# Hybrid decoder layer on one core: two gate blocks kept in SBUF, four product and four x loads moved to SP's queue, reciprocals three steps apart, cross-attention evicted by head pair

## The chip, the core and the metric

The kernel runs on one core of one Trainium2 chip. The core has a matrix engine (TensorE, in the profile PE, with PEld for its weight loads), three engines for elementwise work (VectorE or DVE, ScalarE or ACT, GpSimd or POOL) and SyncE (SP), which in this kernel only issues transfers. Transfers between HBM and the on-chip memory SBUF run on 16 transfer engines, whichever engine issues them. TensorE writes to PSUM, eight banks of 2 KB per partition, from where ScalarE and VectorE read.

The metric is the device time of one execution in microseconds (us). Before the change the median of three runs is 2236.44 us (2235.84 to 2237.41).

## The reference

One decoder layer in float32 over 256 tokens of width 2048: a SwiGLU feed-forward block, a gated mixer of windowed attention and RWKV-7 time mixing, cross-attention into a memory of 256 tokens, and a second feed-forward block. What the change touches:

```python
def gated_parallel_mixer(x, ...):
    p = rms_norm(x, norm_g) @ w_in
    q, k, v, p_rwkv, gates = jnp.split(p, c, axis=-1)
    y_attn = sliding_window_attention(q, k, v, sinks)
    y_rwkv = rwkv7_time_mix(p_rwkv, mu, ...)
    gate_attn, gate_rwkv = jnp.split(jax.nn.sigmoid(gates), 2, axis=-1)
    merged = gate_attn * (y_attn @ w_proj_attn) + gate_rwkv * (y_rwkv @ w_proj_rwkv)
    return x + merged @ w_out

def rwkv7_time_mix(...):
    kk = k * k_k
    kk = kk / jnp.maximum(jnp.sqrt(jnp.sum(kk * kk, axis=-1, keepdims=True)), 1e-12)
    ...

def memory_cross_attention(x, mem, ...):          # 4 heads of 128
    pr = jax.nn.softmax(s, axis=-1)
    o = jnp.einsum('bhtm,bmhd->bthd', pr, vm).reshape(B, T, CROSS_WIDTH)
    return x + o @ w_o
```

## The kernel before

**Products.** Each large product multiplies 256 tokens with a weight matrix in columns of 512. To keep float32 accuracy, every operand is split in a rounded part `hi` and a rest `lo`, and each block is multiplied three times: `hi` by `hi` (L422), weight `lo` by activation `hi` (L423), weight `hi` by activation `lo` (L424). Weights come in blocks of two rows of 128 by 512 columns (512 KB) through four buffers `raw`: SP issues the load (L322), ScalarE casts it to `hi` (L330), VectorE subtracts to get `lo` (L331). Up to four blocks are loaded ahead and two are split ahead. A product with 2048 rows has eight such blocks, one on `yr` has four.

**Background work.** Everything beside the large products is written as generators, kept in named groups (`ew`, `chain`, `norm`, `feat`, `mem` and others). `product` calls `bg.tick()` after every six matmuls, and a tick takes each group's first generators one step further; `yield from idle(n)` lets n ticks pass. So the text of the program interleaves background work with the matmuls. From this text a scheduler makes the order of instructions on each engine and chooses the buffers, so that an instruction may stand ahead of one written earlier.

**The mixer stage.** All its intermediate tiles share 20 buffers of 4 KB per partition (`t4`), among them the halves of `yr`, `mt` and the memory's activations, and the tiles `gr`, `gl`, `ml` and `x2` below. In order of the text: the products for keys; for each of four blocks of 512 columns an attention gate and the projection of the attention's output, whose product is stored to HBM (`md`, L1205); the rows for RWKV; four gate blocks of RWKV (L1520 to L1525), each put through a sigmoid into `gr` and stored to HBM (`grd`); four blocks of the RWKV projection on `yr` (L1535 to L1544), where GpSimd loads back the gate (`gl`, L1537) and the attention's product (`ml`, L1538), and VectorE multiplies and adds them (L1541, L1542); four blocks of the output product (L1558 to L1562), where GpSimd loads a block of x (`x2`, L1559) to which the product is added.

Stores and loads of these tiles are all issued by GpSimd, in its own order; the weights have SP's queue for themselves.

**The key's norm.** `removal_keys(h)` in group `ew`, for each half `h` of the RWKV heads: squares, sums by matmul (L1112), a square root on ScalarE (L1113), then on VectorE a maximum (L1115), four reciprocals of 128x256 (L1117) with two ticks between them (L1118), and the product with `kk` (L1119), followed by a tick (L1120). After it, in the same generator, come the scaled keys (L1123 to L1141) and two blocks of products stored to HBM (L1160). Behind both halves in the same group stands `substitute`, 31 steps of a triangular inverse on VectorE (L1177, L1182), whose result is stored (L1184) and loaded back for `invert` (L1269 to L1273). `chain(h)` and `finish(h)` need it and give `yr`.

**Cross-attention.** The weighted sum over the memory is eight matmuls into one two-bank tile `b4` (L1617 to L1621): for each half of the memory, four heads of 256 columns, so that heads 0 and 1 lie in one bank and 2 and 3 in the other. Then `split` (L634 to L638) is called for each pair of heads: a cast on ScalarE (L636) and a subtraction on VectorE (L637). The product with the output weights needs both.

Of the kernel before, what the change touches and what calls it, by code (L numbers as in the profile page):

```python
# [15 lines left out]
P = 128  # L16
# [124 lines left out]
def decoder_layer(ctx: ExitStack, tc: tile.TileContext, a: dict, out: bass.AP):  # L141
    nc = tc.nc
    act, dve, pool, pe = nc.scalar, nc.vector, nc.gpsimd, nc.tensor
# [17 lines left out]
    def f32(x):  # L161
        return x.bitcast(F32)
# [4 lines left out]
    def two():  # L167
        return ps.tile([P, 2, 512], F32, tag="two", name="two", bufs=2)

    def by_turns(products, late=False):  # L170


        prev = newest["pe"] if late else None
        for to, lhs, rhs, *flags in products:
            how = flags[0] if flags else dict(start=True, stop=True)
            with tc.issue_after(prev.ins) if prev else nullcontext():
                prev = pe.matmul(to, lhs, rhs, **how)  # L177
# [9 lines left out]
    def wait_for(name):  # L187
        while name not in bg.seen:
            yield

    def idle(n):
        for _ in range(n):
            yield
# [86 lines left out]
    for entry in weight_plan(a):  # L280
# [4 lines left out]
        w, k0, nk, c0, n = entry  # L285
# [348 lines left out]
    def split(x: Act, c, n, src):  # L634

        act.copy(x.at(0, c, n), src)  # L636
        dve.tensor_tensor(x.at(1, c, n), src, f32(x.at(0, c, n)), ALU.subtract)  # L637
        x.done |= set(range(c, c + n))  # L638
# [143 lines left out]
    def blk(d, n):  # L782
        return d[:, n * 512 : (n + 1) * 512].rearrange("(t p) n -> p t n", p=P)

    W = {n: v[0] for n, v in a.items() if n not in _LAID}
    x1d = dram.tile([T, D], F32, name="x1d")
    x3d = dram.tile([T, D], F32, name="x3d")
    md = dram.tile([T, D], F32, name="md")
    grd = dram.tile([T, D], F32, name="grd")
# [59 lines left out]
    with tc.tile_pool(name="mx", bufs=1, reuse_waits="tile") as sp:  # L849
        aligned(sp)  # L850

        def t4(name, shape=(P, 4, T), dt=F32):
            return sp.tile(list(shape), dt, tag="t4", name=name, bufs=N4)
# [173 lines left out]
        def halves(x):  # L1027
            return x[:].rearrange("p c (b t) -> p (c b) t", b=2)
# [69 lines left out]
        def removal_keys(h):  # L1098
            yield from wait_for(f"k{h}")
            yield from wait_for("decay")  # L1100
            ei = cs[h]
            kk, sq = t4("kk"), t4("sq")
            for i in range(4):
                c = 4 * h + i
                act.activation(kk[:, i, :], kt[h][:, i, :], AF.Copy, scale=nk_k[:, c : c + 1])
            yield
            act.activation(sq[:], kk[:], AF.Square)
            yield
            b = two()
            v = sq[:].rearrange("p (a c) t -> p a (c t)", a=2)  # L1110
            for i in range(2):
                pe.matmul(b[:, i], bdones[:], v[:, i], start=True, stop=True)  # L1112
            act.activation(v, b[:], AF.Sqrt)  # L1113
            yield
            dve.tensor_scalar(sq[:], sq[:], 1e-12, None, ALU.max)  # L1115
            for i in range(4):
                dve.reciprocal(sq[:, i, :], sq[:, i, :])  # L1117
                yield from idle(2)  # L1118
            dve.tensor_tensor(kk[:], kk[:], sq[:], ALU.mult)  # L1119
            yield  # L1120
            at_.append(t4("at"))
            for later, before in ((slice(1, P), ee[h][:, :, : P - 1]), (0, e0[h][:])):
                dve.scalar_tensor_tensor(  # L1123
                    halves(at_[h])[:, :, later], halves(kk)[:, :, later], DOWN, before,
                    ALU.mult, ALU.mult,
                )
            yield
            dve.scalar_tensor_tensor(kk[:], kk[:], -1.0, aa[h][:], ALU.mult, ALU.mult)
            yield
            dve.tensor_tensor(kk[:], kk[:], ei[:], ALU.mult)  # L1130
            bt.append(kk)
            yield
            for i in range(4):
                c = 4 * h + i
                dve.tensor_scalar(
                    aa[h][:, i, :], aa[h][:, i, :], k_a[:, c : c + 1], ok_a[:, c : c + 1],
                    ALU.mult, ALU.add,
                )
            dve.tensor_tensor(kt[h][:], kt[h][:], aa[h][:], ALU.mult)
            yield  # L1140
            dve.tensor_tensor(aa[h][:], kt[h][:], ei[:], ALU.mult)  # L1141

            for c in range(2):
                cs_ = slice(c * P, (c + 1) * P)
                lt = t4("lt", (P, 8, P))
                b = two()
                by_turns(
                    (
                        b[:, e, j * P : (j + 1) * P], at_[h][64 * e : 64 * e + 64, j, cs_],
                        bt[h][64 * e : 64 * e + 64, j, cs_],  # L1150
                    )
                    for j in range(4) for e in (1, 0)
                )
                yield
                dve.tensor_tensor(
                    lt[:], b[:].rearrange("p e (j s) -> p (e j) s", j=4),
                    mask_l[:].unsqueeze(1).to_broadcast([P, 8, P]), ALU.mult,
                )
                o = h * 16 + c * 8
                pool.dma_start(ld[:, o : o + 8, :], lt[:])  # L1160
                yield
            yield
# [34 lines left out]
        for n in range(4):  # L1197
            pg = product(n2.x, W["w_in"])
            g = t4("ga", (P, 2, 512))
# [317 lines left out]
            bg.spawn("norm", finish(h))  # L1517


        for n in range(4):  # L1520
            pg = product(n2.x, W["w_in"])
            g = t4("gr", (P, 2, 512))
            for t in range(2):
                act.activation(g[:, t, :], pg[t], AF.Sigmoid, scale=n2.r[t])
            pool.dma_start(blk(grd, n), g[:])  # L1525


        mt = act_tiles("mt", 4)
# [1 line left out]
        def merged(m, n):  # L1530
            yield from idle(4)
            split(mt, 4 * n, 4, feats(m))
            yield

        for n in range(4):  # L1535
            g, m = t4("gl", (P, 2, 512)), t4("ml", (P, 2, 512))
            pool.dma_start(g[:], blk(grd, n))  # L1537
            pool.dma_start(m[:], blk(md, n))  # L1538
            pr = product(yr, W["w_proj_rwkv"])
            for t in range(2):  # L1540
                dve.tensor_tensor(g[:, t, :], pr[t], g[:, t, :], ALU.mult)  # L1541
                dve.tensor_tensor(m[:, t, :], g[:, t, :], m[:, t, :], ALU.add)  # L1542
            bg.spawn("feat", merged(m, n))
# [12 lines left out]

        x2 = [t4("x2", (P, 2, 512)) for _ in range(4)]
        for n, s in enumerate(x2):  # L1558
            pool.dma_start(s[:], blk(x1d, n))  # L1559
            po = product(mt, W["w_out"])  # L1560
            for t in range(2):
                dve.tensor_tensor(s[:, t, :], po[t], s[:, t, :], ALU.add)  # L1562
            bg.spawn("feat", n3.block(n, s))
            if n == 0:
                bg.spawn("mem", memory())
# [48 lines left out]
        oc = act_tiles("oc", 1)  # L1614
        b4 = two()[:].rearrange("p a (h t) -> p (a h) t", h=2)
        for mb in range(2):
            for h in range(4):  # L1617
# [1 line left out]
                    b4[:, h], vm[:, mb, h * P : (h + 1) * P], pt[mb][:, h, :],  # L1619
                    start=mb == 0 and h % 2 == 0, stop=mb == 1, skip_group_check=True,  # L1620
                )  # L1621
        for h in (0, 2):
            split(oc, h, 2, b4[:, h : h + 2])
        n4 = Norm(g_ffn2)
        for n in range(4):
            po = product(oc, W["w_cross_o"])
# [110 lines left out]
```

## Time and profile before

| | |
|---|---|
| median of three runs | 2236.44 us (2235.84 to 2237.41) |
| the profiled execution | 2236.75 us |
| its span on the core | 2235.0 us |
| granted TensorE clock over the span | 0.999 |
| read from HBM, written | 420.05 MB, 13.50 MB |

The span goes from the first instruction to the last; the execution's own time is 1.75 us longer. A row of the profile names the engine, the line of the kernel, the operation, the tile written and those read (`out<-in`), and how many such instructions there are. In the timeline a number in brackets is the time that the engine stood idle before the instruction, with what released it. POOL rows with DMA_DIRECT2D are GpSimd issuing a transfer; SPq is SP's queue. The transfers that the change touches, 512 KB each, are in the page's last part and its longer answer:

| transfer | issued by | count | median us to landing |
|---|---|---|---|
| grd<-gr | POOL | 4 | 4.3 |
| gl<-grd | POOL | 4 | 9.7 |
| ml<-md | POOL | 4 | 11.7 |
| x<-x1d | POOL | 4 | 6.5 |
| raw<-in_w_proj_rwkv_dram | SP | 16 | 5.6 |
| raw<-in_w_out_dram | SP | 32 | 3.6 |

### The profile page before, as it was taken

Reading aid. Unit: us, or ns where it says so; the run is one execution under the profiler, and the core shown is the slowest. Engines: PE = TensorE matmul, PEld = TensorE weight load, DVE = VectorE, ACT = ScalarE, POOL = GpSimd, SP = SyncE. Lnnn points to the kernel's source line nnn. Section 1 sums busy time; section 2 is a strip of 40 time slices with the busy share of each in tenths; the row PEclk is TensorE's granted clock in tenths of the full one; section 3 lists DMA queues with packets and bytes.
Section 4 is the critical chain, followed back from the end, with each engine's and each line's share of the span. In section 5 each row is a group of like instructions: output and inputs, shape, how many; then the busy total and the mean of one; then the engine's idle time right before and its main releaser. Section 6 shows DMA issues by size and latency. Waiting matters only on the chain.

```text
span 2235.0 us, 28341 instructions
## 1 busy us (share of the span) xinstructions
PE 2216.0 (99%) x10792; PEld 1819.2 (81%) x10792; DVE 1745.4 (78%) x2039; ACT 1193.5 (53%) x1434; POOL 81.3 (4%) x151
## 2 busy tenths in 40 slices
PE   9999999999999999999999999999999999999998
PEld 7888888888888877788888878888888888888886
DVE  7988988898987567886465466558888888898887
ACT  6555555555555567444443445556555555555554
POOL 1000000000000000103200100001000000000000
PEclk9999999999999999999999999999999999999999
DMA  7666665566556545677435775547665656566664
GB/s 247 211 220 195 203 207 190 187 208 202 194 193 214 165 130 151 219 219 233 121 102 148 230 266 189 181 164 255 201 207 177 218 193 199 193 202 194 207 203 155
DMA packets 219832, 435.40 MB, mean 195 GB/s; under 512 B 13888, under 2 KB 16016, under 8 KB 219696
## 3 DMA queue, kind: packets, MB, share of 16 engines
q1 hardware_dynamic: 210768, 406.37, 56.8%
q0 software_dynamic: 8352, 26.44, 3.8%
q8 instruction: 84, 1.38, 0.3%
q10 hardware_dynamic: 576, 0.79, 0.1%
q14 instruction: 52, 0.43, 0.1%
HBM read 420.05 MB, written 13.50 MB: 194 GB/s over the span
## 4 chain that ended last, share of the span: by engine, by line
PE 93%; DVE 3%; DMA 2%; ACT 1%; issue 1%; SPq 0%; POOLq 0%; POOL 0%; DVEq 0%; ACTq 0%
PE acc L422 20%; PE acc L423 20%; PE acc L424 20%; PE two L422 9%; PE two L423 9%; PE two L424 9%; PE two L185 2%; DVE lo L331 1%; PE two L177 1%; DMA raw<-in_ffn_w_up_dram 1%; DMA raw<-in_w_proj_rwkv_dram 1%; ACT hi L330 0%; PE two L1279 0%; DMA raw<-in_ffn_w_gate_dram 0%; PE acc L1416 0%
## 5 line engine op out<-in xcount | busy, mean ns | idle before, releaser
L330 ACT CAST hi<-raw 128x1024 fp32r<-128x1024 f32 (+1 forms) x770 | 764.2, 1001 | 783.7 <-PE acc L424 362.1
L331 DVE TENSOR_TENSOR lo<-raw,hi 128x1024 fp32r<-128x1024 f32 (+1 forms) x770 | 882.5, 1156 | 343.0 <-ACT hi L330 342.2
L422 PE MATMUL acc<-hi,xhi 128*128 128x512 f32 (+1 forms) x1256 | 491.2, 392 | 1.9 <-ACT hi L330 1.8
L423 PE MATMUL acc<-lo,xhi 128*128 128x512 f32 (+1 forms) x1256 | 488.2, 389 | 2.8 <-DVE lo L331 2.8
L424 PE MATMUL acc<-hi,xlo 128*128 128x512 f32 (+1 forms) x1256 | 486.9, 388 | 0.0
L422 PEld LDWEIGHTS acc<-hi,xhi 128*128 128x128 f32 x1256 | 235.7, 188 | 56.0 <-issue 5.4
L423 PEld LDWEIGHTS acc<-lo,xhi 128*128 128x128 f32 x1256 | 235.9, 188 | 55.2 <-DVE lo L331 6.7
L424 PEld LDWEIGHTS acc<-hi,xlo 128*128 128x128 f32 x1256 | 235.8, 188 | 47.4 <-DVE xlo L680 0.2
L356 DVE TENSOR_TENSOR tlo<-raw,thi 128x1024 fp32r<-128x1024 f32 x160 | 192.8, 1218 | 0.0
L355 ACT CAST thi<-raw 128x1024 fp32r<-128x1024 f32 x160 | 165.7, 1050 | 36.6 <-DVE raw L350 20.1
L423 PE MATMUL acc<-lo,hhi 128*128 128x512 f32 x424 | 166.4, 392 | 0.0
L424 PE MATMUL acc<-hi,hlo 128*128 128x512 f32 x424 | 165.2, 390 | 0.0
L422 PE MATMUL acc<-hi,hhi 128*128 128x512 f32 x424 | 159.8, 391 | 0.0
L422 PE MATMUL two<-hi,xhi 128*128 128x512 f32 x320 | 125.7, 393 | 0.0
L424 PE MATMUL two<-hi,xlo 128*128 128x512 f32 x320 | 124.6, 389 | 0.0
L423 PE MATMUL two<-lo,xhi 128*128 128x512 f32 x320 | 124.6, 389 | 0.0
L350 DVE TENSOR_TENSOR raw<-raw 128x1024 f32<-128x1024 f32 x80 | 97.5, 1219 | 15.4 <-DMA raw<-in_ffn_w_up_dram 13.1
L423 PEld LDWEIGHTS acc<-lo,hhi 128*128 128x128 f32 x424 | 79.6, 188 | 19.4 <-DVE lo L331 3.1
L422 PEld LDWEIGHTS acc<-hi,hhi 128*128 128x128 f32 x424 | 79.1, 188 | 18.6 <-ACT hi L330 2.6
L424 PEld LDWEIGHTS acc<-hi,hlo 128*128 128x128 f32 x424 | 79.6, 188 | 16.2
L422 PEld LDWEIGHTS two<-hi,xhi 128*128 128x128 f32 x320 | 60.1, 188 | 13.4 <-DVE u L574 0.2
L424 PEld LDWEIGHTS two<-hi,xlo 128*128 128x128 f32 x320 | 60.1, 188 | 12.6
(374 smaller groups left out, 3186.2 us busy)
## 6 DMA issues: line engine op xcount, KB each, us to landing
raw<-in_ffn_w_gate_dram SPq DMA_DIRECT2D x167, 512.0 KB, 3.8
raw<-in_ffn_w_up_dram SPq DMA_DIRECT2D x160, 512.0 KB, 4.7
raw<-in_ffn_w_down_dram SPq DMA_DIRECT2D x152, 512.0 KB, 4.8
raw<-in_w_in_dram SPq DMA_DIRECT2D x136, 512.0 KB, 3.7
raw<-in_w_out_dram SPq DMA_DIRECT2D x32, 512.0 KB, 3.6
raw<-in_ffn_w_down_dram SPq DMA_DIRECT2D x12, 1024.0 KB, 5.2
raw<-in_ffn_w_up_dram SPq DMA_DIRECT2D x8, 1024.0 KB, 7.9
raw<-in_w_proj_attn_dram SPq DMA_DIRECT2D x16, 512.0 KB, 4.2
```

The source lines that it names most:

```text
L177: prev = pe.matmul(to, lhs, rhs, **how)
L185: prev = pe.transpose(to, src, ident[:])
L330: newest["act"] = act.copy(hi[:, s], raw[:, s])
L331: newest["dve"] = dve.tensor_tensor(lo[:, s], raw[:, s], f32(hi[:, s]), ALU.subtract)
L350: dve.tensor_tensor(ta[:], raw[:, 1:3], raw[:, 0:2], ALU.subtract)
L355: act.copy(hi[:, s], t[:])
L356: dve.tensor_tensor(lo[:, s], t[:], f32(hi[:, s]), ALU.subtract)
L422: pe.matmul(o, xh, hi, start=first, stop=False, **how)
L423: pe.matmul(o, xh, lo, start=False, stop=False, **how)
L424: newest["pe"] = pe.matmul(o, xl, hi, start=False, stop=last, **how)
```

## The change

Four edits in one function:

- In `removal_keys` the reciprocals are followed by three ticks instead of two, and the product with `kk` by two instead of one.
- Of the four gate blocks, numbers 2 and 3 stay in their tile `gr`; they are neither stored to HBM nor loaded back.
- The loads of `ml` (four) and of `x2` (four) are issued by SP instead of GpSimd.
- In cross-attention the split of a pair of heads is written right behind the last matmul of that pair, so that the first pair's split now stands ahead of the second pair's last two matmuls.

```diff
@@ removal_keys
             for i in range(4):
                 dve.reciprocal(sq[:, i, :], sq[:, i, :])
-                yield from idle(2)
+                yield from idle(3)
             dve.tensor_tensor(kk[:], kk[:], sq[:], ALU.mult)
-            yield
+            yield from idle(2)
@@ gate blocks
+        kept = {}
         for n in range(4):
             pg = product(n2.x, W["w_in"])
             g = t4("gr", (P, 2, 512))
             for t in range(2):
                 act.activation(g[:, t, :], pg[t], AF.Sigmoid, scale=n2.r[t])
-            pool.dma_start(blk(grd, n), g[:])
+            if n < 2:
+                pool.dma_start(blk(grd, n), g[:])
+            else:
+                kept[n] = g
@@ projection of yr
         for n in range(4):
-            g, m = t4("gl", (P, 2, 512)), t4("ml", (P, 2, 512))
-            pool.dma_start(g[:], blk(grd, n))
-            pool.dma_start(m[:], blk(md, n))
+            m = t4("ml", (P, 2, 512))
+            if n in kept:
+                g = kept[n]
+            else:
+                g = t4("gl", (P, 2, 512))
+                pool.dma_start(g[:], blk(grd, n))
+            nc.sync.dma_start(m[:], blk(md, n))
@@ output product
         for n, s in enumerate(x2):
-            pool.dma_start(s[:], blk(x1d, n))
+            nc.sync.dma_start(s[:], blk(x1d, n))
@@ cross-attention
                     start=mb == 0 and h % 2 == 0, stop=mb == 1, skip_group_check=True,
                 )
-        for h in (0, 2):
-            split(oc, h, 2, b4[:, h : h + 2])
+                if mb and h % 2:
+                    split(oc, h - 1, 2, b4[:, h - 1 : h + 1])
```

## The prediction

> **What bounds the kernel now.** I read the page first, then the groups of waits, then the stretches where TensorE waited, each as a timeline by engine.
>
> ```profile
> span 2235.0 us, 28341 instructions
> PE 2216.0 (99%) x10792; PEld 1819.2 (81%) x10792; DVE 1745.4 (78%) x2039; ACT 1193.5 (53%) x1434; POOL 81.3 (4%) x151
> PE 93%; DVE 3%; DMA 2%; ACT 1%; issue 1%; SPq 0%; POOLq 0%; POOL 0%; DVEq 0%; ACTq 0%
> ```
>
> TensorE is the bound: 93% of the chain that ended last is its own work, and no part of the change takes a matmul away. A gain can only come out of the moments in which TensorE's order of matmuls stood still. In the groups of waits the largest such group is matmul L423 on the rest `lo` of a weight block, written by VectorE on L331:
>
> ```profile
> PE acc L423 <- DVE lo L331: 4.7, 8, 1.1
> ```
>
> That is eight times, 4.7 us, 1.1 us at most. The timeline of TensorE shows five of them, in the two places that the change touches (start, duration, engine, line; in brackets the idle time and its releaser):
>
> ```profile
> 889.22 0.61 PE L422 MATMUL acc<-hi,xhi 128*128 128x512 f32 x2
> 890.45 0.50 PE L423 MATMUL acc<-lo,xhi 128*128 128x512 f32 x1 [0.62 <-DVE lo L331]
> ...
> 919.14 0.61 PE L422 MATMUL acc<-hi,xhi 128*128 128x512 f32 x2
> 920.81 0.50 PE L423 MATMUL acc<-lo,xhi 128*128 128x512 f32 x1 [1.06 <-DVE lo L331]
> ...
> 923.25 0.62 PE L422 MATMUL acc<-hi,xhi 128*128 128x512 f32 x2
> 924.14 0.50 PE L423 MATMUL acc<-lo,xhi 128*128 128x512 f32 x1 [0.27 <-DVE lo L331]
> ...
> 1298.70 0.40 PE L424 MATMUL acc<-hi,yr 128*128 128x512 f32 x1
> 1298.95 0.50 PE L422 MATMUL acc<-hi,yr 128*128 128x512 f32 x1
> 1300.21 0.50 PE L423 MATMUL acc<-lo,yr 128*128 128x512 f32 x1 [0.76 <-DVE lo L331]
> ...
> 1302.85 0.43 PE L422 MATMUL acc<-hi,yr 128*128 128x512 f32 x1
> 1304.04 0.50 PE L423 MATMUL acc<-lo,yr 128*128 128x512 f32 x1 [0.77 <-DVE lo L331]
> ```
>
> Matmuls start 0.23 to 0.25 us apart when nothing is late (1298.70 to 1298.95). I count a loss as the distance of two starts less 0.23 for each matmul between. At 889: 890.45 - 889.22 - 2 x 0.23 = 0.77. At 919: 1.21. At 923: 0.43. At 1299: 1.26 - 0.23 = 1.03. At 1303: 1.19 - 0.23 = 0.96.
>
> **Reciprocals a step further apart (L1118, L1120).** The first three losses are VectorE's queue:
>
> ```profile
> 886.00 1.66 DVE L1015 SCALAR_TENSOR_TENSOR kt<-d,v_rwkv,p 128x256 f32<-128x256 f32 x4
> 887.58 1.74 DVE L1117 RECIPROCAL sq<-sq 128x256 f32<-128x256 f32 x1
> 889.24 1.16 DVE L331 TENSOR_TENSOR lo<-raw,hi 128x1024 fp32r<-128x1024 f32 x1
> ...
> 916.33 3.35 DVE L1117 RECIPROCAL sq<-sq 128x256 f32<-128x256 f32 x2
> 919.60 1.16 DVE L331 TENSOR_TENSOR lo<-raw,hi 128x1024 fp32r<-128x1024 f32 x1
> 920.68 1.74 DVE L1117 RECIPROCAL sq<-sq 128x256 f32<-128x256 f32 x1
> ```
>
> A step of the background work is six matmuls, 6 x 0.23 = 1.38 us, and one weight block (two steps, 2.76 us) needs one L331. Today one reciprocal comes per two steps: 1.74 + 1.16 = 2.9 us of VectorE in 2.76 us, before anything else is queued; so `lo` falls behind, at 889 with the four L1015 in front as well, at 919 with two reciprocals back to back. With three steps it is 1.74 + 1.5 x 1.16 = 3.48 us in 4.14 us: VectorE keeps up. Gain at most 0.77 + 1.21 + 0.43 = 2.41; I leave 0.3 of it, since the key's shift work (1.66 us of L1015) still falls between them. At the other end nothing is gained, if the extra steps only put the reciprocals next to other work. I take **-2.1** (bounds -2.4 and 0).
>
> The price is delay: five steps more for each half of the heads, 2 x 5 x 1.38 = 13.8 us later for all that stands behind it in the same group: the products that it stores (L1160), the substitution, and the inverse that GpSimd loads back.
>
> ```profile
> 1015.64 0.59 POOL L1184 DMA_DIRECT2D xd<-xt  x1 [26.11 <-DVE xt L1182]
> ...
> 1048.49 0.10 POOL L1007 MEMSET p<- 128x4 f32 x1 [20.51 <-ACT hi L330]
> ```
>
> GpSimd idles 20.5 us before 1048 and takes up most loads of the inverse only then, so 13.8 us fit in front of it: cost 0. Were that cover gone, the first chain would start up to 13.8 us later; the products on `yr` begin near 1279, some 46 us after the last `yr` was written at 1233, so even then TensorE would not wait.
>
> ```profile
> L637 DVE TENSOR_TENSOR yr<-yq,yr x4: 681/683/685, 1160.0 to 1232.4; 128x512 fp32r<-128x512 f32 x4
> L424 PE MATMUL acc<-hi,yr x64: 387/389/397, 1279.2 to 1327.6; 128*128 128x512 f32 x64
> ```
>
> **Gate blocks kept, loads on SP (L1525 to L1559).** The losses at 1299 and 1303 are late weights:
>
> ```profile
> 1279.98 0.71 POOL L1525 DMA_DIRECT2D grd<-gr  x1 [19.60 <-ACT gr L1524]
> 1280.68 0.71 POOL L1537 DMA_DIRECT2D gl<-grd  x1
> ...
> 1286.38 0.71 POOL L1559 DMA_DIRECT2D x<-x1d  x1
> 1298.00 0.71 POOL L1559 DMA_DIRECT2D x<-x1d  x1 [10.91 <-PE two L185]
> 1328.08 0.71 POOL L1559 DMA_DIRECT2D x<-x1d  x1 [29.37 <-PE acc L424]
> 1335.98 0.71 POOL L1559 DMA_DIRECT2D x<-x1d  x1 [7.20 <-DVE lo L331]
> ```
> ```profile
> 1284.05 13.70 DMA raw<-in_w_proj_rwkv_dram
> ```
> ```profile
> DMA to landing us min/median/max: 3.6/5.1/14.8
> ```
> ```profile
> 1290.00:1295.00 5.00, 5.00 (x24) 4.14 (x23) 2.74 (x5) 1.05 (x1) 0.00 (x0) 1.00 1.02 387
> ```
>
> The first rows are GpSimd's timeline: behind the last gate store (n = 3), three `gl`, three `ml` and one block of x, with the store eight transfers of 512 KB in 6.4 us. The second is from the chain: the weight load issued at 1284.05 took 13.7 us and led to the loss of 1.03. The third is the weight loads of 1270 to 1312 (14 of them): 3.6 at best, 14.8 at worst. The last, the stretches: 387 GB/s with the transfer engines full, so 512 KB take 1.35 us. Eight in front give 3.6 + 8 x 1.35 = 14.4, which fits the worst. A load may take 13.7 - 1.03 = 12.7 us before TensorE notices, so a queue of (12.7 - 3.6) / 1.35 = 6.7 transfers is free.
>
> The change removes two stores and two loads (n = 2, 3), so the store at 1279.98 is gone and the chain "store, then load back" with it. It adds nothing; four `ml` and four x loads move from GpSimd to SP, past the weight loads. If all four `ml` and the first x are issued at once, five stand in front: 10.4 us, under 12.7. With the two `gl` left it is seven: 13.1, 0.4 lost. I take five, since `gl` 0 and 1 no longer wait behind a late store. Gain 1.03 + 0.96 = **-2.0** (bounds -2.0 and 0; a loss is the third rival's). A kept block holds its buffer of the 20 from its sigmoid on, earlier than a reloaded one did; by then `yr` is written and the second chain's tiles are free. Behind each moved load on SP stand the weight loads, and ScalarE and VectorE's split wait for those.
>
> The row of the weight load says that transfers of both queues slow each other. The Trainium skill, "DMA: Bandwidth & Descriptors", section "Issuing engines are not separate DMA queues", says the same as a rule: whichever engine issues, all run on the same 16 DMA engines and interleave. By that rule the move to SP alone gives 0, and only the four transfers removed and the later order help, which is the second rival with the loads' part at 0; the trace agrees that they interleave.
>
> **Cross-attention by pair (L1622).** Timelines of TensorE and ScalarE:
>
> ```profile
> 1492.95 3.61 PE L1618 MATMUL two<-ptm,vm 128*128 128x256 f32 x16
> 1497.24 0.50 PE L422 MATMUL acc<-hi,ochi 128*128 128x512 f32 x1 [0.68 <-ACT ochi L636]
> ```
> ```profile
> 1496.61 0.59 ACT L636 CAST ochi<-two 128x512 fp32r<-128x512 f32 x1 [1.83 <-PE two L1618]
> 1497.95 0.59 ACT L636 CAST ochi<-two 128x512 fp32r<-128x512 f32 x1 [0.76 <-DVE oclo L637]
> ```
>
> TensorE idles 0.68 us for the first cast, which started only when all 16 passes had ended. The edit puts the first split ahead of the last four passes (4 x 0.23 = 0.9 us). If these may run beside it, the 0.68 is gone. But the second cast waited for VectorE's read of the other pair: accesses to this two-bank tile seem to follow each other as a whole. Then the last passes must wait for cast and rest, 0.59 + 0.69 = 1.28 us, and TensorE loses 0.6 more than now unless it runs ready matmuls of the next product meanwhile, which leaves it even. I take **0**, by that nearest row (bounds -0.7 and +0.6).
>
> The Trainium skill speaks for the other reading: "PSUM — Partial Sum Buffer", "Summary: rules for kernel authors", asks to read a different bank than the matmul writes and to guard by bank, and the pairs lie in different banks. By it the sum would be 0.7 lower; the row of the second cast speaks against it.
>
> **Sum.** -2.1 - 2.0 + 0 = -4.1 us. The profiled execution took 2236.75 us (span 2235.0 and 1.75 around it), 0.31 above the median of the runs, 2236.44. Its execution would become 2232.65, the median **2232.3**.
>
> **Rivals.**
> 1. *All of it works.* -2.41 - 1.99 - 0.7 = -5.1: 2231.3. For it: VectorE has room at three steps. Against: the row of the second cast.
> 2. *One of the two stalls stays.* The loads jam again (seven or eight in front), or the reciprocals only move: 2236.4 - 2.1 = 2234.3, or 2236.4 - 2.0 = 2234.4. For it: `ml` and x need no result of this stage, so they can be issued together.
> 3. *Slower: x's loads block the weights.* On GpSimd the last three x loads stood 10.91, 29.37 and 7.20 us for a buffer, with nothing of weight behind them. If they stand so on SP, every weight load waits too. A load normally needs 5.1 us and may need 12.7, so 7.6 are free: 3.3 + 21.8 + 0 = +25.1, giving 2257.4. It decides from one wait of 7.6 + 4.1 = 11.7 us on. Against it: from 1200 to 1480 SP itself stood 196.6 us for VectorE's rests, so it has idle time into which an x load fits once its buffer is free; GpSimd, with nothing else to do, may simply have stood there early.
>
> ```profile
> SPq L322 <- DVE lo L331: 196.6, 77, 8.5
> ```
>
> **How the numbers follow.** Forecast 0.45 (own range 2231.5 to 2233.6); rival 1 0.20; rival 2 0.21; rival 3 0.14. What a measurement tells from no change is about 0.2%, 4.5 us: below 2232.0 counts as faster. Of the forecast 0.18 lies below that, with rival 1 0.38; same is 0.27 + 0.21 = 0.48; slower 0.14. The range goes from 1 us under rival 1 (the order of other instructions may shift by a stall or two of 0.4) to just past no change, 2230.0 to 2237.3, and leaves out rival 3 and little else.
>
> **What would show it.** Reciprocals: no L423 wait over 0.3 us from 870 to 930, and L331 between any two L1117. Loads: no weight load over 12.7 us from 1230 to 1340, no L423 wait near 1300. Cross-attention: whether a cast starts before the last L1618. I am wrong if SP waits for a matmul ahead of a weight load, if a new wait of TensorE turns up from 930 to 1230 where the delayed work now runs, or if the reciprocals still sit in pairs.

## The result and the profile after

The changed kernel takes 2231.11 us (median of 7 runs, 2229.05 to 2232.68), the kernel before, measured beside it, 2236.50 us (7 runs, 2235.84 to 2239.94). The ratio is 0.9973, 95% interval 0.9961 to 0.9984: 5.4 us less by the medians, where 4.1 were forecast. The profiled execution took 2231.27 us. The edit adds some lines: the sigmoid of the gate is now L1525, its store L1527, the load of `gl` L1545, of `ml` L1546, of x L1567, the passes of cross-attention L1626.

From the page after, the shares of the chain that ended last, and from the groups of waits the one of L423 on a rest (sum in us, count, longest):

```profile
PE 98%; DVE 1%; issue 0%; ACT 0%; DMA 0%; SPq 0%; POOLq 0%; POOL 0%; ACTq 0%; DVEq 0%
...
PE acc L423 <- DVE lo L331: 0.8, 1, 0.8
```

TensorE's share of the chain that ended last went from 93% to 98%, and of the eight direct waits of L423 for a rest (4.7 us) one is left, at 21 us, where it stood before too. To see what went where, I summed the losses by stretch, in the way of the prediction: after each matmul of L422 to L424, the distance to the next start less 0.227, where it is over 0.245. (This also counts 0.41 behind each group of four background matmuls of 512 columns, such as L1112, L1239 or L1484, where the matmul that follows them shows no wait. It doesn't count an idle time behind a matmul of another line, such as L1618.)

| stretch, us | before | after | difference |
|---|---|---|---|
| 0 to 860 | 11.94 | 13.52 | +1.6 (of it +1.5 in the first 60) |
| 860 to 960 (reciprocals) | 5.04 | 1.80 | -3.2 |
| 960 to 1250 (substitution, inverse, `yr`) | 6.35 | 5.55 | -0.8 |
| 1250 to 1340 (products on `yr`) | 3.08 | 0.36 | -2.7 |
| 1340 to 1530 (`w_out`, cross-attention) | 1.66 | 1.86 | +0.2 |
| 1530 to the end | 3.14 | 2.90 | -0.2 |

Each kernel has one profile, of one execution. Over the 14 profiles the first 60 us vary between 2.9 and 5.7, with no relation to the edits, so they are left out below.

**VectorE around the reciprocals.** Timeline of VectorE in the second half of the heads, first before (the prediction shows the rows between), then after:

```profile
915.12 0.69 DVE L1115 TENSOR_SCALAR sq<-sq 128x1024 f32<-128x1024 f32 x1 [3.40 <-ACT sq L1113]
915.73 0.68 DVE L1204 TENSOR_TENSOR ga<-acc,ga 128x512 f32<-128x512 f32 x1
...
922.33 0.63 DVE L1204 TENSOR_TENSOR ga<-acc,ga 128x512 f32<-128x512 f32 x1
922.88 1.21 DVE L331 TENSOR_TENSOR lo<-raw,hi 128x1024 fp32r<-128x1024 f32 x1
```

```profile
915.11 1.28 DVE L1204 TENSOR_TENSOR ga<-acc,ga 128x512 f32<-128x512 f32 x2
916.69 1.23 DVE L331 TENSOR_TENSOR lo<-raw,hi 128x1024 fp32r<-128x1024 f32 x1 [0.29 <-ACT hi L330]
919.73 0.69 DVE L1115 TENSOR_SCALAR sq<-sq 128x1024 f32<-128x1024 f32 x1 [1.81 <-ACT sq L1113]
920.45 1.75 DVE L1117 RECIPROCAL sq<-sq 128x256 f32<-128x256 f32 x1
922.12 1.16 DVE L331 TENSOR_TENSOR lo<-raw,hi 128x1024 fp32r<-128x1024 f32 x1
923.20 1.74 DVE L1117 RECIPROCAL sq<-sq 128x256 f32<-128x256 f32 x1
```

The pair of reciprocals is gone, and so are the three waits. But look at the distances: the reciprocals start 2.75 us apart (the next two 2.73 and 2.74), two steps and not three, VectorE doesn't stand idle from the first of them to the last, and TensorE loses nothing there. That is the very load, one reciprocal for each weight block, which the prediction held to be too much. What is new is where they stand: both `ga` multiplications and a rest come ahead of L1115, where before `ga` lay among the reciprocals, one half behind L1115 and the other behind the third reciprocal.

**The queues around `yr`.** SP's four loads of `ml` after, in its timeline (weight loads stand between them), GpSimd's timeline from 1230 on, whole up to 1382, and the landing times of the weight loads issued from 1230 to 1340:

```profile
1273.78 0.41 SPq L1546 DMA_DIRECT2D ml<-md  x1
1276.49 0.42 SPq L1546 DMA_DIRECT2D ml<-md  x1
1295.54 0.41 SPq L1546 DMA_DIRECT2D ml<-md  x1
1307.46 0.37 SPq L1546 DMA_DIRECT2D ml<-md  x1
```
```profile
1234.14 0.73 POOL L1527 DMA_DIRECT2D grd<-gr  x1 [25.46 <-ACT gr L1525]
1234.86 0.74 POOL L1545 DMA_DIRECT2D gl<-grd  x1
1238.50 0.72 POOL L1545 DMA_DIRECT2D gl<-grd  x1 [2.90 <-DMA grd<-gr]
```
```profile
DMA to landing us min/median/max: 3.5/4.5/7.5
```

The burst of eight transfers is gone. SP puts one `ml` at a time between weight loads, 2.7 to 19 us apart, and GpSimd had issued the last of the two `gl` 35 us ahead of the first `ml`. The weight loads took 7.5 us at most, where one had taken 14.8.

**Cross-attention.** TensorE and ScalarE after:

```profile
1487.55 2.75 PE L1626 MATMUL two<-ptm,vm 128*128 128x256 f32 x12
1490.97 0.50 PE L422 MATMUL acc<-hi,ochi 128*128 128x512 f32 x1 [0.68 <-ACT ochi L636]
...
1492.01 1.03 PE L1626 MATMUL two<-ptm,vm 128*128 128x256 f32 x4
```
```profile
1490.34 0.59 ACT L636 CAST ochi<-two 128x512 fp32r<-128x512 f32 x1 [0.97 <-PE two L1626]
```

The first cast now comes after 12 passes instead of 16. The last four did not run beside it: TensorE idles the same 0.68 us for the cast, does four ready matmuls, and issues the four passes at 1492.01, when VectorE's read of the first pair (1490.95, 0.69 us) is over. Nothing is won.

### The profile page after: what moved, and what is told of

It reads as the page before. It is cut to its first block, busy times and chain, and to the rows that moved or that the text cites. A ratio compares the mean times of both kernels' runs of the same rounds, so it can differ in the third digit from the quotient of the medians.

```text
span 2229.6 us, 28331 instructions
## 1 busy us (share of the span) xinstructions
PE 2213.8 (99%) x10792; PEld 1820.2 (82%) x10792; DVE 1747.0 (78%) x2039; ACT 1194.4 (54%) x1434; POOL 71.8 (3%) x139
## 4 chain that ended last, share of the span: by engine, by line
PE 98%; DVE 1%; issue 0%; ACT 0%; DMA 0%; SPq 0%; POOLq 0%; POOL 0%; ACTq 0%; DVEq 0%
PE acc L422 21%; PE acc L423 21%; PE acc L424 21%; PE two L422 9%; PE two L423 9%; PE two L424 9%; PE two L185 2%; PE two L177 1%; PE two L1279 0%; PE acc L1416 0%; DMA raw<-in_ffn_w_gate_dram 0%; PE acc L1398 0%; PE acc L1381 0%; PE two L1495 0%; PE acc L1279 0%
## 5 line engine op out<-in xcount | busy, mean ns | idle before, releaser
L422 PE MATMUL acc<-hi,xhi 128*128 128x512 f32 (+1 forms) x1256 | 492.7, 393 | 2.8 <-ACT hi L330 2.8
L423 PE MATMUL acc<-lo,xhi 128*128 128x512 f32 (+1 forms) x1256 | 488.1, 389 | 0.9 <-DVE lo L331 0.8
L424 PE MATMUL acc<-hi,xlo 128*128 128x512 f32 (+1 forms) x1256 | 487.0, 388 | 0.0
L422 PEld LDWEIGHTS acc<-hi,xhi 128*128 128x128 f32 x1256 | 235.9, 188 | 56.9 <-issue 5.4
L423 PEld LDWEIGHTS acc<-lo,xhi 128*128 128x128 f32 x1256 | 236.4, 188 | 51.7 <-DVE lo L331 3.4
L424 PEld LDWEIGHTS acc<-hi,xlo 128*128 128x128 f32 x1256 | 236.3, 188 | 47.8 <-DVE xlo L680 0.2
L423 PE MATMUL acc<-lo,hhi 128*128 128x512 f32 x424 | 166.4, 392 | 0.0
L424 PE MATMUL acc<-hi,hlo 128*128 128x512 f32 x424 | 165.2, 390 | 0.0
L422 PE MATMUL acc<-hi,hhi 128*128 128x512 f32 x424 | 159.8, 391 | 0.1
L422 PE MATMUL two<-hi,xhi 128*128 128x512 f32 x320 | 125.9, 393 | 0.0
L424 PE MATMUL two<-hi,xlo 128*128 128x512 f32 x320 | 124.6, 390 | 0.0
L423 PE MATMUL two<-lo,xhi 128*128 128x512 f32 x320 | 124.6, 389 | 0.0
L423 PEld LDWEIGHTS acc<-lo,hhi 128*128 128x128 f32 x424 | 79.5, 188 | 19.4 <-DVE lo L331 3.2
L422 PEld LDWEIGHTS acc<-hi,hhi 128*128 128x128 f32 x424 | 79.1, 188 | 18.8 <-ACT hi L330 2.6
L424 PEld LDWEIGHTS acc<-hi,hlo 128*128 128x128 f32 x424 | 79.6, 188 | 16.2
L422 PEld LDWEIGHTS two<-hi,xhi 128*128 128x128 f32 x320 | 60.1, 188 | 13.5 <-DVE u L574 0.2
L424 PEld LDWEIGHTS two<-hi,xlo 128*128 128x128 f32 x320 | 60.1, 188 | 12.6
```

The costliest lines, as they stand in the source:

```text
L422: pe.matmul(o, xh, hi, start=first, stop=False, **how)
L423: pe.matmul(o, xh, lo, start=False, stop=False, **how)
L424: newest["pe"] = pe.matmul(o, xl, hi, start=False, stop=last, **how)
```

## Experiments

Each is the kernel before with the edit named, except where it says "the changed kernel". Times are in us, with before's median in the same series and the ratio's 95% interval (the ratio is not quite that of the two medians). An interval of 0.002 is 4 us wide here, so the sizes are read mainly from the losses by stretch.

| kernel | median (before) | ratio, interval | lost 860 to 960 | 960 to 1250 | 1250 to 1340 |
|---|---|---|---|---|---|
| before | | | 5.04 | 6.35 | 3.08 |
| e1_recips | 2233.03 (2236.22) | 0.9984, 0.9975 to 0.9993 | 1.79 | 5.55 | 2.00 |
| e2_loads | 2234.07 (2236.22) | 0.9991, 0.9982 to 1.0000 | 5.10 | 6.35 | 0.36 |
| e3_cross | 2236.37 (2236.22) | 1.0002, 0.9993 to 1.0011 | 5.10 | 6.34 | 1.83 |
| e4_no_cross | 2230.17 (2236.22) | 0.9973, 0.9963 to 0.9984 | 1.80 | 5.55 | 0.36 |
| e5_kept_only | 2235.24 (2236.18) | 0.9992, 0.9983 to 1.0002 | 5.07 | 6.33 | 0.80 |
| e6_sp_only | 2234.90 (2236.18) | 0.9992, 0.9982 to 1.0001 | 5.04 | 6.34 | 0.36 |
| e7_delay_only | 2232.58 (2236.18) | 0.9981, 0.9972 to 0.9990 | 1.79 | 5.55 | 2.83 |
| e8_two_tiles | 2235.37 (2236.18) | 0.9996, 0.9987 to 1.0006 | 5.02 | 6.35 | 2.07 |
| e9_first_half | 2232.87 (2237.61) | 0.9982, 0.9973 to 0.9990 | 1.68 | 6.72 | 4.56 |
| e10_second_half | 2233.78 (2237.61) | 0.9983, 0.9974 to 0.9991 | 3.23 | 6.77 | 2.03 |
| e11_all_two_tiles | 2228.30 (2237.61) | 0.9964, 0.9950 to 0.9977 | 1.79 | 5.55 | 0.36 |
| e12_ml_together | 2230.77 (2237.61) | 0.9973, 0.9962 to 0.9984 | 1.80 | 5.56 | 0.36 |

### The three parts, each alone, and two together

e1_recips takes the two lines of `removal_keys` from the diff, e2_loads the kept blocks and both moves to SP, e3_cross the split by pair, e4_no_cross the first two together.

> The two tick edits alone. Theory A (VectorE's queue gets room, since a reciprocal now comes per three steps): all L423 waits for the rest between 870 and 945 us go, TensorE's losses there fall from 5.0 us to about 1.8, and the time falls by about 3 us; the losses near 1299 and 1303 (1.03 and 0.96 us) stay as they were. Rival B (the reciprocals only move next to other work): the losses between 870 and 1250 add up to what they were, 11.4 us, and the time stays within 1 us.

> The kept gate blocks and the eight loads on SP alone. Theory A (the queue of transfers at 1280 to 1287 us was the cause): the losses from 1250 to 1340 fall from 3.1 us to about 0.4, no weight load of the projection takes over 7 us, the time falls by about 2.7 us; the losses at 889, 919 and 923 stay (0.77, 1.21, 0.43). Rival B (SP only shares the same transfer engines, the jam stays): weight loads of 13 us and losses of about 1 us each remain near 1299, time within 1 us of before.

> The order of cross-attention alone. Theory A (the two-bank tile is guarded as a whole): TensorE still idles about 0.68 us before the first matmul on the new tile, the last four passes run after VectorE's read of the first pair, in a gap among the next product's matmuls; the time is the same within 0.3 us. Rival B (guarded by bank): the last four passes run beside the first cast, the idle time falls to about 0, and the time falls by 0.7 us.

> The changed kernel with the old order of cross-attention. If the three edits add up and cross-attention is even (theory A): as fast as the changed kernel within 0.3 us, about 5.5 us under the kernel before. If cross-attention did gain (rival B): 0.7 us slower than the changed kernel, about 4.7 us under the kernel before.

By the medians the parts are worth -3.2, -2.2 and +0.2, together -5.2; the first two together gave -6.05 and all three -5.4. So they add, within the intervals, and nothing of the gain needs the third. In e3_cross TensorE stands the same 0.68 us for the first cast as before. In e2_loads the longest weight load took 7.4 us, just over the 7 expected.

One expectation on the losses failed: e1_recips was to leave the losses near 1299 and 1303 as they were, 1.03 and 0.96. Only one of them, 1.03, stayed there, as in e3_cross, though neither kernel touches these loads. Among the seven kernels that keep the old loads, before included, this stretch lost 1.8 to 4.6 us, 2.6 on average. The profiles don't tell whether the kernel or the execution makes that difference.

### Is it the distance between the reciprocals?

e7_delay_only leaves two steps between the reciprocals and puts five steps ahead of them:

```diff
+            yield from idle(5)
             dve.tensor_scalar(sq[:], sq[:], 1e-12, None, ALU.max)
             for i in range(4):
                 dve.reciprocal(sq[:, i, :], sq[:, i, :])
                 yield from idle(2)
```

> The reciprocals keep two steps between them, but five steps pass ahead of them, so that all that follows is as late as in the changed kernel. Theory A (the spacing counts): losses of about 0.4 to 1.2 us in L423 waiting for the rest stay between 870 and 945 us, 2 us or more in all; time within 1.5 us of before. Rival B (it was where they fell, beside the shift work of the keys): the losses go as in the changed kernel, 3 us faster.

The losses from 860 to 960 fell to 1.79, as with the real edit, and those up to 1250 to the same 5.55: rival B. The distance in steps is thus not what is needed. e9_first_half and e10_second_half set the longer distances for one half only:

```diff
-                yield from idle(2)
+                yield from idle(3 if h == 0 else 2)
             dve.tensor_tensor(kk[:], kk[:], sq[:], ALU.mult)
-            yield
+            yield from idle(2 if h == 0 else 1)
```

(e10_second_half with `h == 1`.)

> The kernel before with the longer distances (three steps, two behind the product with kk) for the first half of the heads alone; the second half keeps two and one, but stands behind the first in its group and so comes later. Theory A (what counts is how much work VectorE has queued between two rests, not the distance in steps): the second half's reciprocals come behind the two ga multiplications, one lo between any two, and the losses at 889, 919 and 923 are gone as in the kernel with all of the edit: losses from 860 to 960 about 1.8 us against 5.0, time about 3 to 4 us below before (ratio 0.998 to 0.9985). Theory B (the prediction's: a reciprocal in two steps, 2.9 us in 2.76, is too much for VectorE): the second half, still at two steps, keeps losses of 0.4 us or more near 919 to 926, and only the 0.78 of the first half goes: 860 to 960 at about 3.5 to 4.2 us.

> The kernel before with the longer distances for the second half of the heads alone; the first half is as before. Theory A (work queued between two rests): the loss of 0.78 at 889 stays; in the second half the first two reciprocals no longer stand back to back ahead of a rest, so that rest comes 1.6 us earlier and the losses at 919 and 923 (1.22 and 0.43) go: 860 to 960 at about 3.2 to 3.6 us. Theory B gives the same for the second half. Theory C (the second half must be moved behind the ga multiplications to gain anything): ga still stands among the reciprocals, so 0.4 us or more is left at 919 to 925 and 860 to 960 stays above 4 us. Time by A and B about 1.5 to 2 us below before (ratio 0.9991 to 0.9993), by C under 1.

e9_first_half: 1.68 us are left, theory A. (Its profiled execution, 2236.12 us, is the slowest of its 11, and the old loads cost 4.56 in it; the median is 2232.87.) Its second half still has two steps and only comes later, behind `ga`, as VectorE's timeline shows:

```profile
914.04 1.28 DVE L1204 TENSOR_TENSOR ga<-acc,ga 128x512 f32<-128x512 f32 x2
...
919.38 1.75 DVE L1117 RECIPROCAL sq<-sq 128x256 f32<-128x256 f32 x1
```

e10_second_half: 3.23 us, as A had it. The first half keeps its loss of 0.78 at 889. In the second, `ga` still lies among the reciprocals, but no two of these stand together, and of 1.22 and 0.43 only 0.22 is left (behind the second `ga`, at 921.9), so theory C falls. VectorE's timeline:

```profile
914.92 0.69 DVE L1115 TENSOR_SCALAR sq<-sq 128x1024 f32<-128x1024 f32 x1 [3.40 <-ACT sq L1113]
915.53 0.68 DVE L1204 TENSOR_TENSOR ga<-acc,ga 128x512 f32<-128x512 f32 x1
916.14 1.74 DVE L1117 RECIPROCAL sq<-sq 128x256 f32<-128x256 f32 x1
917.79 1.16 DVE L331 TENSOR_TENSOR lo<-raw,hi 128x1024 fp32r<-128x1024 f32 x1
```

So either way does it. What counts is what VectorE has in its queue between two rests.

ScalarE has a part in the loss at 919 too. Before, it cast this block's `hi` only at 914.98 (1.05 us; the cast ahead was at 909.41), behind the square root L1113, for whose sums it had stood idle 2.30 us. So the rest at 919.60 could not have started before 916.03. e10_second_half has the same late cast (914.79) and loses nothing at 919, so the late cast alone does not stall TensorE.

e10's time fell by 3.8 us, more than the 1.5 to 2 expected; the upper end of its interval, 0.9991, just touches them. Its losses behind the first 60 us fell by 2.6, and 1.05 of that lies from 1250 to 1340, a jam that this edit does not touch and that varies among the kernels with the old loads, as said above.

### Kept blocks or queue?

e5_kept_only keeps gate blocks 2 and 3 but leaves all loads with GpSimd. e6_sp_only moves the loads and keeps nothing.

```diff
-            pool.dma_start(m[:], blk(md, n))
+            nc.sync.dma_start(m[:], blk(md, n))
@@ output product
-            pool.dma_start(s[:], blk(x1d, n))
+            nc.sync.dma_start(s[:], blk(x1d, n))
```

> Only gate blocks 2 and 3 kept on chip; all loads stay on GpSimd. Theory A (fewer transfers in the queue is what counts, whoever issues): with the late store and two reloads gone GpSimd issues its loads earlier and in two groups, no more than five in a row; losses from 1250 to 1340 us fall from 3.1 to under 1, time 2 to 2.5 us lower. Rival B (the queue that issues counts, since SP puts one load between weight loads while GpSimd issues all it may at once): four ml and one x in a row, weight loads over 10 us, at least one loss of 0.5 us or more stays, time within 1.5 us of before.

> Only the eight loads moved to SP; all four gate blocks are stored and loaded back by GpSimd. Theory A (spreading on SP is enough): GpSimd has at most the last store and three gl in a row, 3.6 + 4 x 1.35 = 9 us for a weight load, no loss; losses from 1250 to 1340 fall from 3.1 to about 0.4, as with both edits. Rival B (the store and reload of the last two blocks is needed for the jam): losses over 0.5 us stay.

Each alone takes most of the stall away, in different ways. e5_kept_only, GpSimd's timeline and the weight loads of 1230 to 1310:

```profile
1239.15 0.72 POOL L1527 DMA_DIRECT2D grd<-gr  x1 [26.20 <-ACT hi L330]
1239.87 0.72 POOL L1545 DMA_DIRECT2D gl<-grd  x1
1240.58 0.71 POOL L1546 DMA_DIRECT2D ml<-md  x1
1242.66 0.71 POOL L1545 DMA_DIRECT2D gl<-grd  x1 [1.37 <-DMA grd<-gr]
1243.36 2.11 POOL L1546 DMA_DIRECT2D ml<-md  x3
1245.46 0.71 POOL L1567 DMA_DIRECT2D x<-x1d  x1
```
```profile
DMA to landing us min/median/max: 3.5/4.4/11.9
```

Without the last stores eight transfers still go out in 7 us, in groups of three and five 1.4 us apart, only 40 us earlier. A weight load then took 11.9 us, just under the 12.7 that the prediction had as the limit, and the largest loss in the stretch is 0.19. So theory A has the two groups and the losses (0.80), and rival B the weight loads over 10 us. In e6_sp_only the four stores and four `gl` all remain and GpSimd issues them at most three at a time, while `ml` and x lie in SP's order between the weights; its weight loads took 9.3 us at most and the stretch lost 0.36: theory A.

By time neither is far from before (-0.9 and -1.3 us by the medians, where e5's theory A had 2 to 2.5; both intervals reach 1.0): here the losses decide, not the medians.

e12_ml_together tests the queueing sum. In the changed kernel without its cross-attention edit, SP issues all four `ml` in a row:

```diff
+        mls = []
+        for n in range(4):
+            mls.append(t4("ml", (P, 2, 512)))
+            nc.sync.dma_start(mls[n][:], blk(md, n))
         for n in range(4):
-            m = t4("ml", (P, 2, 512))
+            m = mls[n]
...
-            nc.sync.dma_start(m[:], blk(md, n))
```

> The changed kernel without its cross-attention edit, and with the four loads of ml issued together by SP, in a row ahead of eleven of the sixteen weight loads of the yr projection, in place of one at a time between them. Theory A (the prediction's working: 3.6 us for a load alone, 1.35 more for each transfer of 512 KB in front, 12.7 us before TensorE notices): the weight load behind the four takes 3.6 + 4 x 1.35 = 9.0 us, up to 11.7 with two gl beside them, and nothing is lost: 1250 to 1340 below 0.6 us, time as with one at a time (2229.5 to 2231.5). Rival (SP's own queue adds its wait for a buffer: an ml has to wait for a buffer and the weights behind it wait too, the prediction's third rival): SP stands several us at the ml rows, weight loads are issued late, and 1250 to 1340 loses more than 1.5 us, up to the time of the kernel with the reciprocals alone (2232 to 2233).

SP's timeline, four weight loads and then the four `ml`, and the landing times of the weight loads of 1230 to 1310:

```profile
1263.45 8.53 SPq L322 DMA_DIRECT2D raw<-in_w_proj_rwkv_dram  x4
1272.16 2.08 SPq L1542 DMA_DIRECT2D ml<-md  x4
```
```profile
DMA to landing us min/median/max: 3.5/3.9/9.4
```

The four are issued in 2.1 us without a stand, the worst weight load takes 9.4 us (9.0 by the sum), and the loss is the same 0.36 as with one at a time. Theory A. The rival's case, an x or `ml` load that waits for its buffer with weights behind it, did not come up in any run, so its price remains untried.

### Cross-attention in two tiles

e8_two_tiles gives each pair of heads a tile of one bank and, like e3_cross, splits each pair behind its last matmul, so that against e3_cross only the tiles differ:

```diff
-        b4 = two()[:].rearrange("p a (h t) -> p (a h) t", h=2)
+        b2 = [acc().rearrange("p (h t) -> p h t", h=2) for _ in range(2)]
...
-                    b4[:, h], vm[:, mb, h * P : (h + 1) * P], pt[mb][:, h, :],
+                    b2[h // 2][:, h % 2], vm[:, mb, h * P : (h + 1) * P], pt[mb][:, h, :],
...
+                if mb and h % 2:
+                    split(oc, h - 1, 2, b2[h // 2])
```

> The kernel before with cross-attention's sum in two tiles of one bank each, one per pair of heads, and the split of each pair behind its last matmul. Theory A (the tile was guarded as a whole, so two tiles free the pairs of each other): the first cast starts about 0.9 us before the last pass ends, and TensorE's 0.68 us of idle time goes to under 0.1; time 0.7 us lower. Rival B (the guard is not by tile, or another wait stands there): the idle time stays at 0.68 us.

Timelines of TensorE and ScalarE:

```profile
1491.44 3.61 PE L1618 MATMUL acc<-ptm,vm 128*128 128x256 f32 x16
1494.87 0.50 PE L422 MATMUL acc<-hi,ochi 128*128 128x512 f32 x1
```
```profile
1494.23 0.59 ACT L636 CAST ochi<-acc 128x512 fp32r<-128x512 f32 x1 [0.97 <-PE acc L1618]
```

The first cast starts at 1494.23, while passes are still running (16 of them from 1491.44, 0.22 apart, so the last starts at 1494.68), and L422 follows at 1494.87 with no idle time. The 0.68 us are gone. The time fell by 0.8 us, as large as this, but the interval holds 1.0, so the time alone does not show it.

e11_all_two_tiles is the changed kernel with these tiles.

> The changed kernel with the cross-attention sums in two tiles of one bank, one for each pair of heads, in place of one tile of two banks. Theory A (the guard is on the tile as a whole; with a tile for each bank the first cast runs beside the last passes): the first matmul on ochi follows the passes without the 0.68 us, as in the kernel with this alone, and the time is 0.5 to 0.9 us below the changed kernel, that is 2229.5 to 2230.7 (ratio to before 0.9968 to 0.9973). Rival (the two banks are taken from those of the products, so a product waits for a bank instead): a wait of 0.5 us or more turns up between 1480 and 1500, and the time equals the changed kernel's.

TensorE's first matmul behind the passes, from its timeline:

```profile
1488.78 0.50 PE L422 MATMUL acc<-hi,ochi 128*128 128x512 f32 x1
```

Again no idle time behind the passes and no new wait near by, and 2228.30 us is the lowest median of all kernels, below the 2229.5 to 2230.7 expected: 2.5 us under e12_ml_together of the same series, and with a ratio of 0.9964 where the changed kernel had 0.9973. Only some 0.7 of that is shown to be the tile; the rest is inside the spread of single kernels (the intervals of e11 and e12 overlap).

## Why the prediction was right, and where its steps were not

**The bound.** TensorE's stand-stills were the only thing to win, and they were won: -5.4 us, with -4.1 forecast and rival 1 at -5.1.

**Reciprocals.** The sign and the place were right, the main step of the mechanism was wrong, and the term too small. The step that failed is "today one reciprocal comes per two steps: 1.74 + 1.16 = 2.9 us of VectorE in 2.76 us ... so `lo` falls behind". Durations of neighbouring instructions overlap by 0.08 us; from start to start a reciprocal takes 1.66 (884.92 - 883.26 before) and a rest 1.08 (886.00 - 884.92), together 2.74, and a block of 12 matmuls takes TensorE 12 x 0.227 = 2.72. Both the changed kernel and e9_first_half run at that for a whole half and lose nothing. One reciprocal per block is about the most that fits, and what breaks it is anything more in the same place, as the prediction also said of the four L1015 and of the two reciprocals back to back. Before, that was a second reciprocal, L1115 and half of `ga` ahead of the rest at 919.60, and the other half ahead of the rest at 922.88. For the first half the count is the same. Before, from the rest at 878.32 to that at 889.24, VectorE did three rests, three reciprocals and the key's L1011 and L1015 in 10.92 us, 3.64 per block. VectorE's timeline after, first half:

```profile
880.01 2.29 DVE L331 TENSOR_TENSOR lo<-raw,hi 128x1024 fp32r<-128x1024 f32 x2
882.22 1.75 DVE L1117 RECIPROCAL sq<-sq 128x256 f32<-128x256 f32 x1
883.88 1.16 DVE L1011 TENSOR_TENSOR d<-p 128x1024 f32<-128x1024 f32 x1
884.96 1.22 DVE L331 TENSOR_TENSOR lo<-raw,hi 128x1024 fp32r<-128x1024 f32 x1
886.09 1.67 DVE L1015 SCALAR_TENSOR_TENSOR kt<-d,v_rwkv,p 128x256 f32<-128x256 f32 x4
887.68 1.75 DVE L1117 RECIPROCAL sq<-sq 128x256 f32<-128x256 f32 x1
889.34 2.29 DVE L331 TENSOR_TENSOR lo<-raw,hi 128x1024 fp32r<-128x1024 f32 x2
```

Four rests (two, one, and the first of the next two) but two reciprocals from 880.01 to about 890.4: 2.6 per block, and the rests run one ahead when L1015 comes.

So there was luck in the term. In the second half the edit did not space the reciprocals, it only moved them, which rival 2 held to be worth nothing; they moved behind both halves of `ga`, and e7_delay_only, with no more distance at all, gains as much.

The size: the three losses named (0.77, 1.21, 0.43) are all gone, so -2.4 and not -2.1. Two more of the same generator, which are among the prediction's eight waits but not in its sum, went with them: 0.38 at 906 and 0.36 at 942. In both places steps of `removal_keys` stood in a row ahead of rests that were due. VectorE's timeline before, at the first:

```profile
901.89 1.21 DVE L1155 TENSOR_TENSOR lt<-two,mask_l 128x1024 f32<-128x1024 f32 x1
903.03 1.21 DVE L1141 TENSOR_TENSOR aa<-kt,cs 128x1024 f32<-128x1024 f32 x1
904.16 1.21 DVE L1155 TENSOR_TENSOR lt<-two,mask_l 128x1024 f32<-128x1024 f32 x1
905.29 3.56 DVE L331 TENSOR_TENSOR lo<-raw,hi 128x1024 fp32r<-128x1024 f32 x3
```

After, a rest stands between them (908.61, between two L1155). With that the stretch gives -3.2. The other -0.8, up to 1250, comes with e1_recips and e7_delay_only alike and not with e9 or e10; half of it is one delay of 0.41 fewer behind background matmuls (three such groups of four in the stretch, before four). Why is open.

**The delay at no cost.** Right. GpSimd stores the inverse 14.05 us later (1029.69, before 1015.64), of its 20.51 us of idle time ahead of L1007 7.23 are left, and the last `yr` is no later: 1229.8 against 1232.4. GpSimd's row of that store and the group of VectorE's rows that write `yr` (count, ns, first and last start), both after:

```profile
1029.69 0.59 POOL L1184 DMA_DIRECT2D xd<-xt  x1 [8.27 <-DVE xt L1182]
...
L637 DVE TENSOR_TENSOR yr<-yq,yr x4: 683/685/692, 1183.9 to 1229.8; 128x512 fp32r<-128x512 f32 x4
```

The cover was less complete than the prediction had it, though. GpSimd issues its last load from `xd` at 1104.8 (before 1073.5), and the first `yr` is written 23.9 us later than before (1160.0), more than the 13.8 that the prediction allowed without any cover. It cost nothing because the products on `yr` begin only near 1276, behind both halves.

**Loads.** The term -2.0 was mis-sized by little: the stretch lost 2.7 us less, and alone the edit gave -2.2 by time. But the loss before differs from profile to profile, so the two losses in the sum, 1.03 and 0.96, were partly luck: against the 2.6 that the old loads cost on average, 0.36 is 2.3 less. The sum for the queue held where the transfers stand in a row in one queue (9.4 us measured for 9.0 in e12_ml_together). Elsewhere it is only a rough guide: three transfers in front of a weight load in e6_sp_only make 7.7 and 9.3 were measured, and the eight of e5_kept_only would make 14.4, like the eight before, and 11.9 were measured. Its fit to 14.8 had luck in it too: the gate store that it counts had landed by 1284.99, when the `gl` that waited for it went out, while the worst load went out only at 1286.77, with two weight loads still under way in front of it. The limit of 12.7 held as far as tried: 11.9 lost almost nothing. The step "four `ml` and the first x are issued at once, five stand in front" was wrong to the safe side: on SP they stand between weight loads in the order of the queue, so hardly more than one is in front. That is also why the second rival did not come about. By the rule of the Trainium skill, "DMA: Bandwidth & Descriptors", section "Issuing engines are not separate DMA queues", the prediction had put the move to SP alone at nothing. e6_sp_only had the move alone and 0.36 left of 3.08. The transfers do share the engines, as the rule says; but the issuing queue decides when a transfer starts, and GpSimd, with nothing else to do, had started them all at once. Rival 3 lost on the point that the prediction named against it: SP stood nowhere at an `ml` or x row.

**Cross-attention.** Right at 0, and by the mechanism that it took: the tile of two banks is guarded as a whole. The last four passes waited for cast and rest, and four ready matmuls filled part of that, "which leaves it even". The rule to guard by bank (the Trainium skill, "PSUM — Partial Sum Buffer", "Summary: rules for kernel authors") holds too once there is a tile for each bank: e8_two_tiles and e11_all_two_tiles win the 0.68.

**The sum.** By stretches -3.2 - 0.8 - 2.7 + 0.2 = -6.5, measured -5.4 with -8.7 to -3.6 by the interval of the ratio. The forecast's -4.1 lies in it; what it missed are the two small losses (0.7), the part from 960 to 1250 (0.8), 0.7 of the jam and 0.3 that it had held back of the first three losses.

## What to carry to other kernels

Where a queue feeds the bound engine at a fixed beat, sum from start to start, not by durations, and count for each stretch between two due instructions everything that stands ahead of the second; a wait is cured by moving any of it, and a distance in steps is only one way to do so. When a load is late, ask who issues the transfers in front of it and what paces that engine: an idle queue sends them in one burst, a queue shared with the weights paces them. If two halves of a PSUM tile are to be written and read at the same time, make them two tiles.

## What the runs showed that was not expected

- VectorE can run one reciprocal of 128x256 and one rest of 128x1024 every 2.73 us without idle time, though their durations sum to 2.9: each starts some 0.08 us before the record of the one ahead ends (a rest at 922.12, the reciprocal ahead of it recorded from 920.45 to 922.20).
- Five steps ahead of the reciprocals did not move the first one of the first half (876.48 in e7_delay_only, 876.64 before), but the third by 3.7 us (886.95, before 883.26), behind the key's L1015: the order on the engine, not the count of steps, is what must be read.
- Eight transfers of 512 KB in 7 us delayed a weight load to 11.9 us in e5_kept_only and to 14.8 before. The loss was 0.19 us at most in the one and over 1 us in the other: near the limit of 12.7, two or three microseconds of a load decide over the whole stall.
